# The first norm of a one-layer hybrid encoder: loads, weight splits and tensor work in a new order

## The chip, the cores and the metric

The kernel runs on one core of a Trainium2 chip. The metric is device time in microseconds (us) of one execution; it is given as the median of three runs. A hardware profile of one further execution gives the trace: what each engine did and when, and what ended each wait. The engines are PE (TensorE matmul; PEld is its weight load), ACT (ScalarE), DVE (VectorE), POOL (GpSimd) and SP (SyncE, which here only issues loads and stores). PE's clock has two levels, 1.2 and 2.4 GHz, which the profile shows as a granted clock of 0.50 and 1.00.

## What is computed

512 prompt tokens and 64 sample tokens with 1024 channels go through one transformer-like layer. The change touches only its beginning:

```python
def ada_modulation(c, w_ada, b_ada):
    mod = jax.nn.silu(c) @ w_ada + b_ada           # 6 vectors of 1024 for prompt, 6 for sample
    return jnp.split(mod[:, None, :], 6, axis=-1)  # sh1, sc1, g1, sh2, sc2, g2

h = rms_norm(x, norm1_g) * (1 + sc1) + sh1
q, k, v, qi, ki, wi, ga, gb = jnp.split(h @ w_in, PROJ_SPLITS, axis=-1)
u = ga * jax.nn.sigmoid(gb)                        # feeds a causal depthwise convolution, width 31
```

What follows is sparse attention with an indexer, the convolution, an output projection, a second norm and a squared-ReLU MLP of width 4096.

## The kernel before

All 576 tokens are held at once, channels on the partitions, in eight tiles `hat` of 128 channels. Weights keep fp32 accuracy by a split: `hi` is the rounded weight (an ACT copy, L106) and `lo` the rest (a subtraction, L115, on DVE or POOL); activations `h` are split in the same way, and each product is three matmuls (hi by hi, lo by hi, hi by lo) of 288 columns.

The first stage, up to about 58 us, does the first norm and the first three products. In order:

- Five token tiles `xtok` are loaded. `rms` takes each one's mean square (ACT, L261, L262) and scales it (DVE, L263, L264); `turn_in` transposes it on PE (L272) into `hat`. `columns` brings the conditioning vectors and the small parameter rows into columns (L214, L218).
- The shift and scale of the norm come in five blocks of channels (`BLOCKS`: 2, 2, 2, 1 and 1 tiles of 128). `load_block(b)` loads four `ada` tiles of `w_ada`, `mod_steps` multiplies them (L234), copies the result (`modrow`, L106), sums and turns it (L241) and finishes it on DVE (L248, L251). `front(b)` is a generator that does this and then, one tile at a time, `modulate(k)`: `h` hi on ACT (L283), the full value on DVE (L284), `h` lo on DVE (L115).
- `products(k, m...)` multiplies `h` tile k with weight m (L415): m = 0 is the indexer key `ki` (72 columns), m = 1 the gate `gb0`, m = 2 the value `ga0`. There are 8 x 3 such products of 6 matmuls each; below, (k, m) names one. `first_w(m, eng)` makes the split of weight m.
- `conv_setup` turns the convolution's taps (`small`) on PE (L426, L431) and copies them out.

PE, ACT and DVE run in the order in which the code is written (a manual schedule); POOL's order was left to a scheduler. All loads go through SP's queue in program order. Eight semaphores serve SP's loads in turn, so a load is issued only when the one eight places ahead of it has landed. The `ada` tiles rotate through `ADA` = 10 buffers, the `xtok` tiles have buffers of their own. The order of the stage is written out by hand: `step` takes a list in which an integer b advances `front(b)` by one step and a tuple (k, m...) runs `products`.

Behind the stage, `evac_ki` (L110, L106, L115) and the gate (`sig` L533, `u` L538) empty the six result banks, and the taps of the first convolution group, `yc` on DVE (L562, L564), start from `u`. `wraw`, `whi` and `wlo` are the weights of the products that follow (L290 to L292), split by `split`.

Of the kernel before, what the change touches and what calls it, by code (L numbers as in the profile page):

```python
# [7 lines left out]
FT = mybir.dt.float32  # L8
# [4 lines left out]
OP = mybir.AluOpType  # L13
AX = mybir.AxisListType

D = 1024
# [15 lines left out]
NP_ = 4  # L32
KP = FF // 128 // NP_
W = 31
ADA = 10
VEC, PEC = (0, 3), (1, 2)

P = dict(PRW=30, TPE=5, CS0=43, KYW=5, TAP=2, T0=20, IDX=2, TKS=12, ATT=4, SMP=6, MOD=21, CPW=15, MODL=6, S0=4, KEYW=5, TAPW=8, SCW=14, MODW=20, QIW=6, CSW=16, TKW=9, TK2=2, TKP=2, ATW=6, SMW=6, TT=3, CN1=8, CN2=21, CN3=8, RT=3, CNW=17)
HALO = W - 1
# [4 lines left out]
EPS = 1e-6  # L44
# [27 lines left out]
def step_kernel(ctx: ExitStack, tc: tile.TileContext, io):  # L72
    nc = tc.nc
    act, dve, pool, pe = nc.scalar, nc.vector, nc.gpsimd, nc.tensor

    def new_pool(stack, name, bufs=1):
        return stack.enter_context(tc.tile_pool(name=name, bufs=bufs, reuse_waits="tile"))

    cst = new_pool(ctx, "cst")
# [15 lines left out]
    def p_lg():  # L95
        return bank("lg", 2)

    def p_tp():
        return bank("tp", 2)
# [21 lines left out]
    def xtile(i):  # L121
        return (x_p[128 * i:128 * i + 128], 128) if i < 4 else (x_s, SAMP)

    start = ExitStack()
    stp = new_pool(start, "start")

    rows = stp.tile([128, 128], FT, name="rows")
    crow = stp.tile([16, 128], FT, name="crow")
    for s, ap in enumerate((io["c_prompt"], io["c_sample"])):
# [3 lines left out]
    xt = []  # L133
    for i in range(5):
        src, n = xtile(i)
        t = stp.tile([128, D], FT, name=f"xtok{i}")
        nc.sync.dma_start(t[:n], src)
        xt.append((t, n))
        for r, ap in parts[2 * i:2 * i + 2]:
            k = ap.shape[1] // 128  # L140
            nc.sync.dma_start(rows[r:r + k, :], ap.rearrange("o (n c) -> (o n) c", c=128))

    BLOCKS = ((0, 2), (2, 2), (4, 2), (6, 1), (7, 1))

    def load_block(b):
        f0, nf = BLOCKS[b]
        tiles = []
        for v in range(2):
            for kh in range(2):
                t = stp.tile([128, 4, 256], FT, name="ada", tag="ada", bufs=ADA)[:, :, :128 * nf]  # L150
                c0 = 1024 * v + 128 * f0
                nc.sync.dma_start(t, w_ada[512 * kh:512 * kh + 512, c0:c0 + 128 * nf].rearrange("(k p) c -> p k c", p=128))
                tiles.append(t)
        return tiles
# [3 lines left out]
    def load_w(name, src, r0, c0, n=128):  # L158
        raw = wgt.tile([128, NK, 128], FT, name="wraw", tag="wraw", bufs=3)
        nc.sync.dma_start(raw[:, :, :n], src[r0:r0 + 1024, c0:c0 + n].rearrange("(k p) c -> p k c", p=128))  # L160
        wraw[name] = (raw, n)
# [8 lines left out]
        return hi, lo, n  # L170

    small = stp.tile([128, 2, 512], FT, name="small")
    pool.memset(small[:, 0], 0.0)
    pool.memset(small[:64, 1], 0.0)
    ada = [load_block(0)]
    load_w("ki", w_in, 0, C_KI, 72)
    for s in range(4):
        n = 8 if s < 3 else 7
        nc.sync.dma_start(small[32 * s:32 * s + n, 0], io["conv_w"][0][s:s + 4 * n - 3:4])
    nc.sync.dma_start(small[:W, 1], io["conv_w"][0])  # L180
    nc.sync.dma_start(small[32:32 + HALO, 1], io["state_conv"][0, 0])
    load_w("gb0", w_in, 0, C_GB)
    ada.append(load_block(1))
    load_w("ga0", w_in, 0, C_GA)
    for b in (2, 3, 4):
        ada.append(load_block(b))


    begin = ExitStack()
    begin.enter_context(tc.manual_schedule(engines={mybir.EngineType.PE, mybir.EngineType.Activation, mybir.EngineType.DVE}))  # L190
    ident = cst.tile([128, 128], FT, name="ident")
    par = cst.tile([128, 128], FT, name="par")
    ones = cst.tile([128, 128], FT, name="ones")
    onec = cst.tile([128, 128], FT, name="onec")
    eps = cst.tile([128, 1], FT, name="eps")
    jp = stp.tile([128, 128], FT, name="jp")
    pool.iota(jp, pattern=[[1, 128]], base=0, channel_multiplier=-1, allow_small_or_imprecise_dtypes=True)
    dve.tensor_scalar(ident, jp, 0.0, None, op0=OP.is_equal)
    pa = mt([128, 128], FT, "pa")
    dve.tensor_scalar(pa, jp, 64.0, None, op0=OP.is_equal)  # L200
    dve.tensor_scalar(par, jp, -64.0, None, op0=OP.is_equal)
    dve.tensor_tensor(par, par, pa, op=OP.add)
    dve.tensor_tensor(par, par, ident, op=OP.add)
    pool.memset(ones, 1.0)
    pool.memset(onec, 1.0 / 512.0)
    pool.memset(eps, EPS)

    cs = cst.tile([128, NK, 32], FT, name="cs")
    pool.memset(cs, 0.0)
    cols = cst.tile([128, 128], FT, name="cols")  # L210

    def columns():
# [179 lines left out]
    def first_w(m, eng):  # L392
        hl = [stp.tile([128, NK, 128], FR, name=f"fw{m}{z}") for z in range(2)]
        fw[m] = split_w(("ki", "gb0", "ga0")[m], *hl, eng=eng)
# [28 lines left out]
    def conv_setup():  # L423
        t = p_tp()
        for c in range(4):
            pe.transpose(t[:, 64 * c:64 * c + 64], small[:64, 1, 128 * c:128 * c + 128], ident[:64, :64])  # L426
        tv = t[:, :256].rearrange("p (c j) -> p c j", c=4)
        t = p_lg()
        for b in range(16):
            for s in range(4):  # L430
                pe.matmul(t[32 * s:32 * s + 32, 8 * b:8 * b + 8], lhsT=small[:, 0, 32 * b:32 * b + 32],  # L431
                          rhs=ident[:, 32 * s:32 * s + 8], start=True, stop=True, tile_position=(0, 32 * s), skip_group_check=True)
        yield
        copy_to(act, cw, tv[:, :, :W])
        copy_to(act, us[:, :, :HALO], tv[:, :, 32:32 + HALO])
        copy_to(act, wcol, t[:, :128])
        dve.tensor_tensor(i4, ident[:, 0:32], ident[:, 32:64], op=OP.add)
        dve.tensor_tensor(i4, i4, ident[:, 64:96], op=OP.add)
        dve.tensor_tensor(i4, i4, ident[:, 96:128], op=OP.add)
# [12 lines left out]
    def step(*todo):  # L452
        if not banks:
            banks.extend([p_acc(), p_acc(), p_acc(), p_lg(), p_lg(), p_av()])
        for e in todo:
            if isinstance(e, int):
                next(fr[e])
            else:
                products(*e)

    next(fr[0])
    first_w(0, pool)
    next(fr[0])
    setup = conv_setup()
    next(setup)
    first_w(1, pool)
    step((0, 0), 0)
    next(setup, None)
    step((1, 0), (0, 1))
    first_w(2, dve)  # L470
    step(1, (1, 1), 1, 1, (0, 2), (1, 2), (2, 0, 1, 2), (3, 0))
    step(2, (3, 1), 2, 3, 2, (3, 2), 3, (4, 0, 1, 2))
    fetch()
    fetch()
    ckr = big.tile([128, 8, 2, 64], FT, name="ckr", tag="b")
    for s in range(2):
        nc.sync.dma_start(ckr[:, :, s, :], io["cache_kidx"][0, 0].rearrange("(n p) d -> p n d", p=128))
    step(4, (5, 0), 4)
    split()
    step((5, 1), (5, 2), (6, 0), (7, 0))  # L480
    for j in range(2):
        evac_ki(j, banks[j][:, :HALF], JS[j])
    step((6, 1), (7, 1), (6, 2), (7, 2))
# [821 lines left out]
    for part in range(NP_ - 1):  # L1305
        a_ = first_layer(part)
        for m in range(NK):
# [3 lines left out]
            else:  # L1311
                for r in JS:
                    t = p_ff()[:, :HALF]
# [45 lines left out]
    for m in range(2, NK):  # L1359
        ws.append(weight())  # L1360
        t = p_ff()[:, :320]
# [49 lines left out]
```

## Time and profile before

| What | Value |
|---|---|
| Median of 3 runs | 861.04 us (860.79 to 861.17) |
| The profiled execution | 860.36 us |
| Its span, first to last instruction | 858.6 us |
| PE busy | 808.2 us, 94% of the span |
| DVE, ACT, POOL busy | 449.0, 412.5, 303.5 us |
| Granted PE clock, mean | 0.973 |
| DMA, mean | 111 GB/s |

The span is what the trace covers; the profiled execution is 1.8 us longer than its span and 0.7 us shorter than the median. A busy PE is not a PE at its peak: at the lower clock it is as busy with half the work.

### The profile page before, as it was taken

What the parts mean: (1) busy time and instruction counts of PE and PEld (TensorE: products, weight loads), DVE (VectorE), ACT (ScalarE), POOL (GpSimd) and SP (SyncE); (2) the same over time, 40 slices, a digit from 0 to 9 for tenths busy, and PEclk for the clock granted to TensorE, in tenths of its full rate; (3) what the DMA queues carried; (4) which work ended last, traced back from release to release, by engine and by line L of the source; (5) the groups of instructions that cost most, each with busy time, mean ns of one, the idle gap of its engine ahead of it and who ended that gap; (6) DMA issues with size and microseconds to landing.
All of it is one profiled execution on the core that took longest, in us unless ns stands there. A gap on an engine that the chain in (4) does not pass through costs nothing.

```text
span 858.6 us, 17186 instructions
## 1 busy us (share of the span) xinstructions
PE 808.2 (94%) x6787; PEld 753.0 (88%) x6787; DVE 449.0 (52%) x1148; ACT 412.5 (48%) x976; POOL 303.5 (35%) x337
## 2 busy tenths in 40 slices
PE   5998997989798999999999999999999999999995
PEld 3797895567777988989999999999999999999995
DVE  4569879999997444654934311343113321144142
ACT  5365554555776787754745411443224522244332
POOL 0146342222244414232424343343433343343800
PEclk8799999899999999999999999999999999999998
DMA  8984157247343343732222323223222323223312
GB/s 241 309 205 123 53 146 184 60 100 187 112 113 110 116 137 115 222 122 77 74 74 75 97 76 93 80 75 99 74 77 82 88 83 90 74 74 101 120 55 57
DMA packets 164555, 95.57 MB, mean 111 GB/s; under 512 B 7699, under 2 KB 161119, under 8 KB 164475
## 3 DMA queue, kind: packets, MB, share of 16 engines
q1 hardware_dynamic: 164475, 94.48, 39.2%
q8 instruction: 53, 0.87, 0.4%
q14 instruction: 27, 0.22, 0.1%
HBM read 88.82 MB, written 5.64 MB: 110 GB/s over the span
## 4 chain that ended last, share of the span: by engine, by line
PE 69%; DVE 17%; ACT 7%; DMA 3%; issue 3%; POOL 1%; SPq 0%; ACTq 0%; DVEq 0%; POOLq 0%
PE ps_acc L290 11%; PE ps_acc L291 11%; PE ps_acc L292 11%; PE ps_lg L292 5%; PE ps_lg L290 5%; PE ps_lg L291 5%; DVE yc L564 3%; PE ps_av L292 3%; PE ps_av L290 2%; PE ps_av L291 2%; DVE score L690 2%; DVE m L688 2%; PE ps_tp L234 2%; DMA ada<-w_ada 1%; PE ps_av L887 1%
## 5 line engine op out<-in xcount | busy, mean ns | idle before, releaser
L332 POOL TENSOR_TENSOR wlo<-wraw,whi 128x512 fp32r<-128x512 f32 x172 | 222.6, 1314 | 378.3 <-ACT whi L106 378.0
L290 PE MATMUL ps_acc<-h,whi 128*128 128x288 f32 (+1 forms) x608 | 190.8, 314 | 0.0
L291 PE MATMUL ps_acc<-h,whi 128*128 128x288 f32 (+1 forms) x608 | 181.7, 299 | 0.0
L292 PE MATMUL ps_acc<-h,wlo 128*128 128x288 f32 (+1 forms) x608 | 181.1, 298 | 0.0
L106 ACT ACTIVATE whi<-wraw 128x512 fp32r<-128x512 f32 x172 | 99.8, 621 | 126.4 <-issue 120.6
L290 PEld LDWEIGHTS ps_acc<-h,whi 128*128 128x128 f32 x608 | 116.2, 191 | 14.3 <-issue 12.4
L291 PEld LDWEIGHTS ps_acc<-h,whi 128*128 128x128 f32 x608 | 116.7, 192 | 0.8
L292 PEld LDWEIGHTS ps_acc<-h,wlo 128*128 128x128 f32 x608 | 116.3, 191 | 0.0
L1266 ACT ACTIVATE z<-z,bs 128x224 f32<-128x224 f32 (+2 forms) x96 | 40.2, 450 | 98.6 <-DVE z L1262 98.6
L1087 DVE SCALAR_TENSOR_TENSOR x<-ps_acc,mod,x 128x288 f32<-128x288 f32 (+3 forms) x91 | 36.2, 420 | 83.6 <-PE ps_acc L292 83.0
L564 DVE SCALAR_TENSOR_TENSOR yc<-u,cw,yc 128x606 f32<-128x606 f32 x60 | 58.4, 981 | 0.6
L292 PE MATMUL ps_acc<-a,wlo 128*128 128x288 f32 x192 | 56.7, 295 | 0.0
L290 PE MATMUL ps_acc<-a,whi 128*128 128x288 f32 x192 | 56.6, 295 | 0.0
L291 PE MATMUL ps_acc<-a,whi 128*128 128x288 f32 x192 | 56.6, 295 | 0.0
L292 PE MATMUL ps_lg<-h,wlo 128*128 128x288 f32 (+1 forms) x176 | 52.2, 296 | 0.8 <-POOL wlo L332 0.8
L291 PE MATMUL ps_lg<-h,whi 128*128 128x288 f32 (+1 forms) x176 | 52.2, 297 | 0.0
L290 PE MATMUL ps_lg<-h,whi 128*128 128x288 f32 (+1 forms) x176 | 52.2, 296 | 0.1
L747 ACT ACTIVATE gc<-sful,sg 128x544 bf16<-128x544 f32 x48 | 35.8, 746 | 28.6 <-DVE sg L745 27.8
L872 POOL TENSOR_SCALAR prob<-prob,mx 128x128 f32<-128x128 f32 (+3 forms) x32 | 20.2, 631 | 56.8 <-DVE mx L871 34.2
L1087 DVE SCALAR_TENSOR_TENSOR x<-ps_lg,mod,x 128x64 f32<-128x64 f32 (+4 forms) x34 | 12.7, 407 | 52.5 <-PE ps_lg L292 52.5
L292 PE MATMUL ps_lg<-a,wlo 128*128 128x288 f32 x128 | 37.8, 295 | 0.0
L290 PE MATMUL ps_lg<-a,whi 128*128 128x288 f32 x128 | 37.8, 295 | 0.0
(358 smaller groups left out, 2019.0 us busy)
## 6 DMA issues: line engine op xcount, KB each, us to landing
wraw<-w_ff SPq DMA_DIRECT2D x64, 512.0 KB
ada<-w_ada SPq DMA_DIRECT2D x44, 512.0 KB
wraw<-w_in SPq DMA_DIRECT2D x24, 512.0 KB
wraw<-w_out SPq DMA_DIRECT2D x8, 512.0 KB
rep<-ud SPq DMA_DIRECT2D x24, 115.0 KB
xtok<-x_prompt SPq DMA_DIRECT2D x4, 512.0 KB
ada<-w_ada SPq DMA_DIRECT2D x8, 256.0 KB
ct<-cache_k SPq DMA_DIRECT2D x8, 256.0 KB
```

The costliest lines, as they stand in the source:

```text
L106: act.activation(out, in_, AF.Copy, scale=1.0 if scale is None else scale)
L234: pe.matmul(t[r:r + 32, :w], lhsT=cs[:, 4 * kh + kk, :], rhs=operand(v, kh, kk), start=kk == 0, stop=kk == 3, tile_position=(0, r))
L290: pe.matmul(out, lhsT=hi, rhs=src[:, 0, cs_], start=first, stop=False)
L291: pe.matmul(out, lhsT=hi, rhs=src[:, 1, cs_], start=False, stop=False)
L292: pe.matmul(out, lhsT=lo, rhs=src[:, 0, cs_], start=False, stop=last)
L332: behind[0] = pool.tensor_tensor(lo[:, c], raw[:, c], f(hi[:, c]), op=OP.subtract).ins
L564: dve.scalar_tensor_tensor(yc[c], src, w, yc[c], op0=OP.mult, op1=OP.add)
L688: dve.max(m, score[i])
L747: act.activation(eq, sful, AF.Sign, bias=cands[:, z:z + 1], scale=-1.0, accum_out=cnts[:, z:z + 1])
L872: pool.tensor_scalar(pt[:, :n], pt[:, :n], m[:, 1:2], 1.0, op0=OP.mult, op1=OP.mult)
L1087: dve.scalar_tensor_tensor(xm[:, a:b], t[:, a - r.start:b - r.start], mod[:, g, s, m:m + 1], xm[:, a:b], op0=OP.mult, op1=OP.add)
L1266: act.activation(y, y, AF.Relu, bias=bs[:, s:s + 1])
```

## The change

Everything is in the first stage. The constants (`ident`, `ones` and others) are made first, and POOL joins the engines that run in written order. The `xtok` tiles share the `ada` buffers, of which there are now 15. Parameter rows and convolution taps are loaded through POOL's queue. `gb0` is loaded directly behind `ki`. All three first weights are split on DVE. `conv_setup` moves from the beginning to between the last products of tile 4 and the first of tile 5, and takes its second bank from `p_tp`. A helper `warm(n)` runs n matmuls of `ones` by `ones` whose result nobody reads. The list of steps is written anew.

```diff
-ADA = 10
+ADA = 15
...
-    begin.enter_context(tc.manual_schedule(engines={mybir.EngineType.PE, mybir.EngineType.Activation, mybir.EngineType.DVE}))
+    begin.enter_context(tc.manual_schedule(engines={mybir.EngineType.PE, mybir.EngineType.Activation, mybir.EngineType.DVE,
+                                                     mybir.EngineType.Pool}))
...
-        t = stp.tile([128, D], FT, name=f"xtok{i}")
+        t = stp.tile([128, D], FT, name=f"xtok{i}", tag="ada", bufs=ADA)
         nc.sync.dma_start(t[:n], src)
         xt.append((t, n))
         for r, ap in parts[2 * i:2 * i + 2]:
             k = ap.shape[1] // 128
-            nc.sync.dma_start(rows[r:r + k, :], ap.rearrange("o (n c) -> (o n) c", c=128))
+            pool.dma_start(rows[r:r + k, :], ap.rearrange("o (n c) -> (o n) c", c=128))
...
     ada = [load_block(0)]
     load_w("ki", w_in, 0, C_KI, 72)
-    for s in range(4):
-        n = 8 if s < 3 else 7
-        nc.sync.dma_start(small[32 * s:32 * s + n, 0], io["conv_w"][0][s:s + 4 * n - 3:4])
-    nc.sync.dma_start(small[:W, 1], io["conv_w"][0])
-    nc.sync.dma_start(small[32:32 + HALO, 1], io["state_conv"][0, 0])
     load_w("gb0", w_in, 0, C_GB)
     ada.append(load_block(1))
     load_w("ga0", w_in, 0, C_GA)
     for b in (2, 3, 4):
         ada.append(load_block(b))
...
+    for s in range(4):
+        n = 8 if s < 3 else 7
+        pool.dma_start(small[32 * s:32 * s + n, 0], io["conv_w"][0][s:s + 4 * n - 3:4])
+    pool.dma_start(small[:W, 1], io["conv_w"][0])
+    pool.dma_start(small[32:32 + HALO, 1], io["state_conv"][0, 0])
...
-        t = p_lg()
+        t = p_tp()
         for b in range(16):
             for s in range(4):
                 pe.matmul(t[32 * s:32 * s + 32, 8 * b:8 * b + 8], lhsT=small[:, 0, 32 * b:32 * b + 32],
...
+    def warm(n):
+
+        t = p_tp()
+        for _ in range(n):
+            pe.matmul(t[:, :128], lhsT=ones, rhs=ones, start=True, stop=True)
+
+    first_w(0, dve)
     next(fr[0])
-    first_w(0, pool)
+    warm(3)
     next(fr[0])
+    warm(6)
+    first_w(1, dve)
+    step((0, 0), 0)
+    first_w(2, dve)
+    step((0, 1, 2), 1, (1, 0), 1, 1, (1, 1, 2), (2, 0, 1, 2), 2, (3, 0), 2, 2, (3, 1, 2), (4, 0), 3, (4, 1), 3, (4, 2))
     setup = conv_setup()
     next(setup)
-    first_w(1, pool)
-    step((0, 0), 0)
+    step((5, 0))
     next(setup, None)
-    step((1, 0), (0, 1))
-    first_w(2, dve)
-    step(1, (1, 1), 1, 1, (0, 2), (1, 2), (2, 0, 1, 2), (3, 0))
-    step(2, (3, 1), 2, 3, 2, (3, 2), 3, (4, 0, 1, 2))
+    step(4)
...
-    step(4, (5, 0), 4)
+    step((5, 1, 2), 4, (6, 0), (7, 0))
     split()
-    step((5, 1), (5, 2), (6, 0), (7, 0))
```

Three places show how the order moves. First SP's queue in the kernel before, from the last token tile on (`ada` are tiles of the blocks, `wraw` with 72 columns is `ki`, the next two `wraw` are `gb0` and `ga0`):

```order
L137 DMA xtok_94<-x_sample 64x1024
L152 DMA ada<-w_ada 128x4x256 x4
L160 DMA wraw<-w_in 128x8x72
L179 DMA small<-conv_w 8x512 x3
L179 DMA small<-conv_w 7x512
L180 DMA small<-conv_w 31x512
L181 DMA small<-state_conv 30x512
L160 DMA wraw<-w_in 128x8x128
L152 DMA ada<-w_ada 128x4x256 x4
```

The same place in the changed kernel:

```order
L158 DMA xtok_112<-x_sample 64x1024
L173 DMA ada<-w_ada 128x4x256 x4
L181 DMA wraw<-w_in 128x8x72
L181 DMA wraw<-w_in 128x8x128
L173 DMA ada<-w_ada 128x4x256 x4
```

The six loads of taps that stood between `ki` and `gb0` have gone to POOL's queue; `ga0` still stands behind block 1. Second, PE from block 0's modulation to block 1's in the kernel before (fw_295 and fw_296 are hi and lo of `ki`, fw_382 and fw_383 those of `gb0`):

```order
L234 MATMUL ps_tp<-ada,cs 32x256 x16
L241 MATMUL ps_tp<-sel,modrow 128x4 x2
L426 MATMUL ps_tp<-ident,small 128x64 x4
L431 MATMUL ps_lg<-ident,small 32x8 x64
L415 MATMUL ps_acc<-h,fw_295 72x288
...
L415 MATMUL ps_acc<-h,fw_382 128x288
L415 MATMUL ps_acc<-h,fw_383 128x288
...
L234 MATMUL ps_tp<-ada,cs 32x256 x16
```

In the changed kernel fw_276 and fw_277 are `ki`, fw_323 and fw_324 `gb0`, fw_346 and fw_347 `ga0`:

```order
L235 MATMUL ps_tp<-ada,cs 32x256 x16
L466 MATMUL ps_tp<-ones 128x128 x3
L242 MATMUL ps_tp<-sel,modrow 128x4 x2
L466 MATMUL ps_tp<-ones 128x128 x6
L416 MATMUL ps_acc<-h,fw_276 72x288
...
L416 MATMUL ps_lg<-h,fw_346 128x288
L416 MATMUL ps_lg<-h,fw_347 128x288
L416 MATMUL ps_av<-h,fw_346 128x288
...
L235 MATMUL ps_tp<-ada,cs 32x256 x16
```

The setup is gone from here, the `ones` matmuls are in, and `ga0` is now read before block 1's modulation, where it was first read after it. Third, PE around the setup's new place, from the last `ga0` product of tile 4 to the last block's turning:

```order
L416 MATMUL ps_av<-h,fw_346 128x288
L427 MATMUL ps_tp<-ident,small 128x64 x4
L432 MATMUL ps_tp<-ident,small 32x8 x64
L416 MATMUL ps_acc<-h,fw_276 72x288
...
L235 MATMUL ps_tp<-ada,cs 32x128 x16
...
L242 MATMUL ps_tp<-sel,modrow 128x4
```

All three products of tile 5 now stand ahead of that last turning; in the kernel before, only its `ki` product did, and no setup stood there.

## Rows read from the trace of the kernel before

**Rows 1.** The profile's page, part 1: busy time, share of the span, instructions.
```profile
PE 808.2 (94%) x6787; PEld 753.0 (88%) x6787; DVE 449.0 (52%) x1148; ACT 412.5 (48%) x976; POOL 303.5 (35%) x337
```
**Rows 2.** Stretches: PE, PEld, DVE, ACT, POOL busy (count); PE clock, DMA share, GB/s.
```profile
2.50:13.50 11.00, 5.36 (x24) 4.70 (x24) 4.27 (x11) 6.38 (x15) 0.18 (x1) 1.00 0.96 267
13.50:17.50 4.00, 2.52 (x20) 1.70 (x18) 3.48 (x8) 3.94 (x10) 0.00 (x0) 0.95 1.09 348
...
19.50:21.00 1.50, 1.50 (x16) 0.78 (x20) 0.00 (x0) 0.00 (x0) 0.00 (x0) 0.50 0.42 103
...
19.50:33.30 13.80, 11.99 (x180) 8.40 (x180) 6.44 (x12) 4.55 (x10) 3.84 (x2) 0.50 1.00 304
...
24.00:34.00 10.00, 8.67 (x161) 7.05 (x165) 6.44 (x12) 4.38 (x10) 3.84 (x2) 0.50 1.09 341
34.50:58.00 23.50, 23.50 (x258) 20.97 (x251) 13.42 (x36) 12.32 (x25) 3.89 (x4) 1.00 0.83 215
...
61.00:98.00 37.00, 32.48 (x240) 30.36 (x238) 36.14 (x53) 17.93 (x43) 20.96 (x34) 0.95 0.48 130
```
**Rows 3.** PE's timeline: start, us, line, out<-in, count, idle time before it and releaser.
```profile
13.93 0.28 PE L218 MATMUL ps_tp<-ident,rows 76*128 76x76 f32 x1
...
19.49 3.62 PE L234 MATMUL ps_tp<-ada,cs 128*32 128x256 f32 x26 [0.57 <-DMA ada<-w_ada]
...
24.53 0.69 PE L426 MATMUL ps_tp<-ident,small 64*128 64x64 f32 x4
25.14 1.89 PE L431 MATMUL ps_lg<-ident,small 128*32 128x8 f32 x128
26.97 2.28 PE L415 MATMUL ps_acc<-h,fw 128*72 128x288 f32 x8
...
33.35 2.31 PE L234 MATMUL ps_tp<-ada,cs 128*32 128x256 f32 x32
...
38.52 0.96 PE L415 MATMUL ps_acc<-h,fw 128*72 128x288 f32 x6
...
41.84 1.93 PE L234 MATMUL ps_tp<-ada,cs 128*32 128x256 f32 x32
```
**Rows 4.** ACT's timeline, same columns.
```profile
25.64 1.15 ACT L283 ACTIVATE h<-hat,mod 128x512 fp32r<-128x512 f32 x2 [1.54 <-DVE mod L251]
...
33.32 1.06 ACT L106 ACTIVATE fw<-wraw 128x1024 fp32r<-128x1024 f32 x1 [4.07 <-DMA wraw<-w_in]
...
53.41 2.18 ACT L106 ACTIVATE whi<-wraw 128x512 fp32r<-128x512 f32 x4
...
58.83 0.41 ACT L533 ACTIVATE sig<-ps_lg 128x288 f32<-128x288 f32 x1
```
**Rows 5.** DVE's timeline, same columns.
```profile
27.50 2.80 DVE L284 TENSOR_SCALAR hfull<-hat,mod 128x512 f32<-128x512 f32 x2
...
34.41 1.22 DVE L115 TENSOR_TENSOR fw<-wraw,fw 128x1024 fp32r<-128x1024 f32 x1 [2.69 <-ACT fw L106]
...
37.48 0.77 DVE L284 TENSOR_SCALAR hfull<-hat,mod 128x512 f32<-128x512 f32 x2
...
51.90 0.23 DVE L248 TENSOR_TENSOR mod<-ps_tp,cols 128x2 f32<-128x2 f32 x2 [0.40 <-PE ps_tp L241]
...
61.22 1.09 DVE L562 TENSOR_SCALAR yc<-u,cw,cols 128x606 f32<-128x606 f32 x1
```
**Rows 6.** POOL's timeline, same columns.
```profile
27.82 2.44 POOL L115 TENSOR_TENSOR fw<-wraw,fw 128x1024 fp32r<-128x1024 f32 x1 [2.23 <-ACT fw L106]
```
**Rows 7.** SP's timeline, same columns: the issue of `gb0`'s load.
```profile
19.46 0.39 SPq L160 DMA_DIRECT2D wraw<-w_in  x1
```
**Rows 8.** PE's timeline after an idle stretch later in the program.
```profile
84.85 0.44 PE L622 MATMUL ps_lg<-kip,qi 128*128 128x384 f32 x1 [1.70 <-ACT relu L625]
...
85.97 0.44 PE L290 MATMUL ps_acc<-h,whi 128*128 128x288 f32 x1
...
89.37 0.29 PE L290 MATMUL ps_acc<-h,whi 128*128 128x288 f32 x1
```

More of the change, by code (lines that the diff above doesn't have):

```diff
@@ L125, in step_kernel @@
     stp = new_pool(start, "start")
+    begin = ExitStack()
+    begin.enter_context(tc.manual_schedule(engines={mybir.EngineType.PE, mybir.EngineType.Activation, mybir.EngineType.DVE,
+                                                     mybir.EngineType.Pool}))
+    ident = cst.tile([128, 128], FT, name="ident")
+    par = cst.tile([128, 128], FT, name="par")
+    ones = cst.tile([128, 128], FT, name="ones")
+    onec = cst.tile([128, 128], FT, name="onec")
+    eps = cst.tile([128, 1], FT, name="eps")
+    jp = stp.tile([128, 128], FT, name="jp")
+    pool.iota(jp, pattern=[[1, 128]], base=0, channel_multiplier=-1, allow_small_or_imprecise_dtypes=True)
+    dve.tensor_scalar(ident, jp, 0.0, None, op0=OP.is_equal)
+    pa = mt([128, 128], FT, "pa")
+    dve.tensor_scalar(pa, jp, 64.0, None, op0=OP.is_equal)
+    dve.tensor_scalar(par, jp, -64.0, None, op0=OP.is_equal)
+    dve.tensor_tensor(par, par, pa, op=OP.add)
+    dve.tensor_tensor(par, par, ident, op=OP.add)
+    pool.memset(ones, 1.0)
+    pool.memset(onec, 1.0 / 512.0)
+    pool.memset(eps, EPS)
     rows = stp.tile([128, 128], FT, name="rows")
@@ L172, in step_kernel @@
     small = stp.tile([128, 2, 512], FT, name="small")
-    pool.memset(small[:, 0], 0.0)
-    pool.memset(small[:64, 1], 0.0)
     ada = [load_block(0)]
     load_w("ki", w_in, 0, C_KI, 72)
-    for s in range(4):
-        n = 8 if s < 3 else 7
-        nc.sync.dma_start(small[32 * s:32 * s + n, 0], io["conv_w"][0][s:s + 4 * n - 3:4])
-    nc.sync.dma_start(small[:W, 1], io["conv_w"][0])
-    nc.sync.dma_start(small[32:32 + HALO, 1], io["state_conv"][0, 0])
     load_w("gb0", w_in, 0, C_GB)
@@ L186, in step_kernel @@
         ada.append(load_block(b))
-    begin = ExitStack()
-    begin.enter_context(tc.manual_schedule(engines={mybir.EngineType.PE, mybir.EngineType.Activation, mybir.EngineType.DVE}))
[L191 to L206, printed above, removed]
     cs = cst.tile([128, NK, 32], FT, name="cs")
     pool.memset(cs, 0.0)
+    pool.memset(small[:, 0], 0.0)
+    pool.memset(small[:64, 1], 0.0)
+    for s in range(4):
[3 more added lines that the diff above has]
+    pool.dma_start(small[32:32 + HALO, 1], io["state_conv"][0, 0])
     cols = cst.tile([128, 128], FT, name="cols")
```

## The prediction

> **What bounds the kernel now.** The page's first part says that PE is busy 94% of the span [rows 1]. That is a mean, and the change lies in the first 58 us, so I read that stretch alone: first the stretches, then the timelines of PE, ACT and DVE.
>
> The stretches [rows 2] show three regimes. From 2.5 to 13.5 us the token tiles arrive at 267 GB/s with a DMA share of 0.96; from 13.5 to 17.5 us block 0 comes at 348 GB/s with a share of 1.09. Then there is a hole: from 19.5 to 21 us 103 GB/s and a share of 0.42. The queue explains it: between `ki` and `gb0` stand six small loads of taps, and `gb0` is issued only at 19.46 us [rows 7], with block 1 behind it. From 24 to 34 us the rate is 341 GB/s again. From 34.5 to 58 us PE is busy 23.50 of 23.50 us at the full clock. So up to about 33 us the stage is bound by what has landed, and from there by PE.
>
> PE's timeline [rows 3] gives the marks. Block 0's modulation waits for its last tile until 19.49. The convolution setup runs from 24.53 to 27.03 (0.69 and 1.89 us, at clock 0.50). The first product starts at 26.97, and the `h` that it reads was made by ACT from 25.64 for 1.15 us, to 26.79 [rows 4]: the setup filled a wait and cost some 0.2 us. Block 1's modulation starts at 33.35, and then PE never rests. `ga0` has landed at 33.32, where ACT stops waiting for it [rows 4], and its lo part is ready at 35.63 (34.41 plus 1.22) [rows 5]; PE has other work until then.
>
> What the stage hands on is not PE's last product but the last tile's modulation. It starts when DVE gets the last sums, at 51.90 [rows 5]. From there ACT makes `h`, splits weights (53.41), empties banks and gates, up to `sig` at 58.83, which ends at 59.24 [rows 4], and DVE starts the taps `yc` at 61.22 [rows 5]. From 61 to 98 us DVE is busy 36.14 of 37.00 us, while PE has 4.5 us idle [rows 2]. So a delay of the mark at 51.90 goes through DVE into the end almost whole. I forecast that mark.
>
> **The change part by part.** *Constants first, buffers, POOL's order.* The first token tile lands after the constants are made in either order, so this is worth nothing on the path. The 15 buffers hold the five token tiles and ten block tiles, as many block tiles as before; the eleventh now waits for a token tile that has long been used, not for block 0's matmuls. That moves blocks 2 to 4 forward, which PE did not wait for: nothing.
>
> *Small loads on POOL's queue.* They are 0.23 MB, and 11 of them were on SP between the first token tile and `gb0`. No row shows a load issued by POOL. The parameter rows are needed by PE at 13.93 [rows 3]; the six issues start at about 2 us, so even 1.5 us each leaves room: I take nothing, with a loss of 1 us at most if they come late. The tap loads are not needed until the setup, some 20 us later than before.
> The Trainium skill, page "DMA: Bandwidth & Descriptors", section "Issuing engines are not separate DMA queues", says that loads from different engines run on the same 16 DMA engines and that a second issuer saves only issue time. By it the 0.23 MB still cost what they did, and only the hole at 19.5 us, which is an issue wait, would go. The trace shows that hole, and shows no overlap of two issuers.
>
> *When `ga0` lands.* Order behind the token tiles: block 0, `ki` (0.29 MB), `gb0` (0.52), block 1 (2.10), `ga0` (0.52). Block 0 was complete at 19.49. Without small loads between the token tiles, at most the lacking share (0.96 against 1.09, 12% of 11 us, 1.3 us) is won: it lands at 18.2 to 19.5, and I take 18.9. Behind it come 3.43 MB. At 348 GB/s they take 9.9 us. At the slow end, in the kernel before 304 GB/s for 13.8 us moved 4.20 MB up to `ga0`, where 3.6 were ahead of it: 0.6 MB of later tiles overtook. With these too, at 341 GB/s, it is 11.8 us [rows 2]. I take 10.6, nearer the fast end, since part of the overtaking comes from the hole. So `ga0` lands at 29.5, between 28.1 and 31.3: some 3.8 us earlier than before.
>
> *The new wait.* PE now reads `ga0` with tile 0, ahead of block 1's modulation. By then it has done (0, 0) and most of (0, 1), so it stands. Behind the waiting matmul on PE is all that is left; on ACT behind the copy of `ga0` stands block 1's `modrow`, on DVE behind the subtraction stand block 1's sums. After landing, the copy takes 1.06 and the subtraction 1.22 us [rows 4, 5], 2.3 together. PE goes on in full at 31.8.
>
> *What PE has to do up to the mark.* Before, from 33.35 to 51.90, 18.55 us without a pause: four modulations, four turnings, and 78 of the 144 product matmuls (18 were done, 48 left). After, from 31.8: the same four and four, but 97 product matmuls, 7 left of tile 0 and all 90 of tiles 1 to 5. 24 of them and nothing else ran from 38.52 to 41.84, 0.138 us each [rows 3], so the 19 more cost 2.6 us. The setup now stands in a full stretch: 2.5 us at the half clock before, 1.25 if all of it scales; I take 1.6. At (4, 0) the lo part comes late by some 0.3 us, since only 12 matmuls (1.66 us) stand between the turning and it, and the way through DVE and ACT takes 2.4. Against that, block 1's modulation ran 2.31 us where block 2's ran 1.93, the rest of a low clock: 0.4 less. Sum: 18.55 + 2.6 + 1.6 + 0.3 - 0.4 = 22.65. The mark comes at 31.8 + 22.65 = 54.45, which is 2.55 us late.
>
> *What is taken off.* POOL's splits go (2.44 us for `gb0` [rows 6]), and with them the DVE step beside them of 2.80 us that takes 0.77 elsewhere [rows 5]. This delayed tile 1, which now waits for `ga0` anyway: no gain left. `warm` puts nine matmuls around block 0's turning; they end before `ga0` lands: no cost, and PE's clock is likely up by then.
>
> *Behind the mark*, (7, 0) has only (6, 0) in front and PE stands about 1 us; ACT's chain is longer, so it costs nothing more.
>
> **Sum.** 860.36 + 2.55 = 862.9 for the profiled execution; the median is 0.7 above it, so 863.6. With `ga0` at 28.1 it is 862.2, at 31.3 it is 865.4; a setup of 1.25 or 2.5 us moves it by -0.35 or +0.9.
>
> **Rivals.** *The loads ran slowly because of how they were issued, and now run at full rate from the start: faster.* From the start of the token tiles at 2.5 us, 7.84 MB up to `ga0` at 348 GB/s end at 25.0. For it speaks the rate between 13.5 and 17.5, against it the share of 0.96 up to 13.5: the DMA engines were busy, only slow. The mark then comes at 25.0 + 2.3 + 22.65 = 49.95, 1.95 early: 859.1. No change is reached with `ga0` at 27.0, and 0.2% is gained from 25.2 down. Chance 0.18.
>
> *Both sides cancel.* `ga0` between 25.2 and 28.6, the order's loss eaten by the closed hole: 861.0. For it speaks that the hole is plain in the rows. Chance 0.27.
>
> *The clock falls while PE waits for `ga0`.* PE stands for some 2 to 3 us around 29 to 32. Later in the program, after an idle time of 1.70 us, its 288-column matmuls take 0.44 instead of 0.29 us from 84.85 until before 89.37 [rows 8]: at most 4.5 us at the lower level of the clock, a loss of at most 2.2, and I take 1.8. Here that comes on top: 865.4. Against it, that stretch had more idle time around it than the one row shows. Chance 0.17.
> The Trainium skill, page "TensorE: Matmul & The Clock Gate", section "HAM oscillation — how this bites in real kernels", tells of this: a wait for a load lets the clock fall, and the next work starts slow. The trace agrees at 84.85 us, with 0.44 against 0.29 us [rows 8].
>
> **How the numbers follow.** The forecast has 0.38, the three rivals 0.18, 0.27 and 0.17. 0.2% of 861 is 1.7 us, about what a measurement of this kernel can tell from no change, so slower begins at 862.8 and faster ends at 859.3. Slower takes the third rival and 0.35 of the forecast, 0.52; faster takes nearly all of the first, 0.17; the same is left with 0.31. The likeliest case alone lies between 862.2 and 865.4. Eight in ten need both neighbours: from 859.8, which leaves out most of the first rival, to 866.0.
>
> **What the changed profile would show.** Right: no hole of DMA before block 1, and 300 GB/s or more between block 0 and `ga0`; ACT's wait for `ga0` ends near 29.5; PE idle 2 to 3 us in front of the first `ga0` products; the setup in 1.3 to 2 us at full clock; the last block's sums on DVE at 54 to 55, `yc` at about 63.8. Wrong: `ga0` landed by 27, no idle time of PE there, the mark at or before 52, or DVE not full from 61 to 98, so that the delay is swallowed.

## The result and the profile after

The changed kernel takes 867.62 us, median of four executions (867.17 to 868.48), the kernel before 861.11 in the same series: ratio 1.0076, 95% interval 1.0059 to 1.0094. It is slower by 6.5 us, where 2.5 were forecast; the range ended at 866.0. The profiled execution is the one of 868.48 us, span 866.7.

The page's first part, as [rows 1], and the stretches that answer to [rows 2], same columns; the last one is 61 to 98 us moved by the 6.1 us that DVE is late:

```profile
PE 808.0 (93%) x6805; PEld 752.5 (87%) x6805; DVE 446.4 (52%) x1150; ACT 412.9 (48%) x976; POOL 307.4 (35%) x347
```
```profile
2.50:13.50 11.00, 5.59 (x26) 5.23 (x27) 4.90 (x10) 7.73 (x18) 6.94 (x14) 1.00 1.05 309
...
19.50:21.00 1.50, 1.50 (x24) 0.73 (x13) 0.22 (x1) 0.83 (x2) 0.00 (x0) 1.00 1.18 295
19.50:30.30 10.80, 5.97 (x54) 4.23 (x42) 5.35 (x11) 4.20 (x7) 0.00 (x0) 0.86 1.12 331
24.00:34.00 10.00, 3.40 (x14) 2.42 (x13) 4.35 (x6) 2.71 (x4) 0.00 (x0) 0.67 1.11 338
...
67.10:104.10 37.00, 30.67 (x238) 28.68 (x236) 36.14 (x53) 17.85 (x41) 22.08 (x36) 1.00 0.49 131
```

The loads did better: 309 GB/s up to 13.5 us (267 before), and the hole at 19.5 us is closed (295, was 103). But PE did 14 matmuls between 24 and 34 us, at a mean clock of 0.67; it had done 161 there, 132 of them the setup's small ones. DVE is as full behind the stage as it was: 36.14 of 37 us. PE's timeline shows the place:

```profile
18.90 1.91 PE L235 MATMUL ps_tp<-ada,cs 128*32 128x256 f32 x26 [0.92 <-DMA ada<-w_ada]
...
26.17 0.42 PE L416 MATMUL ps_lg<-h,fw 128*128 128x288 f32 x2
31.42 0.61 PE L416 MATMUL ps_lg<-h,fw 128*128 128x288 f32 x1 [4.83 <-ACT fw L106]
32.68 0.61 PE L416 MATMUL ps_lg<-h,fw 128*128 128x288 f32 x1 [0.65 <-DVE fw L115]
...
34.66 3.36 PE L235 MATMUL ps_tp<-ada,cs 128*32 128x256 f32 x32
...
43.36 1.93 PE L235 MATMUL ps_tp<-ada,cs 128*32 128x256 f32 x32
...
52.51 0.46 PE L427 MATMUL ps_tp<-ident,small 64*128 64x64 f32 x4
52.89 1.26 PE L432 MATMUL ps_tp<-ident,small 128*32 128x8 f32 x128
```

Block 0 is complete at 18.90. Then PE stands 4.83 us for ACT's copy of `ga0` and 0.65 us for its lo part, and what follows runs at the lower clock (granted 1.00 from 21 to 27.3 us, 0.50 from 27.4 to 37.6): the first matmul takes 0.61 us (0.40 in e3 below, at the full clock), block 1's modulation 3.36, block 2's, with as many matmuls, 1.93. ACT's and DVE's rows, as [rows 4, 5]: `ga0` landed at 30.31, its lo part, and the mark (the last block's sums) with what starts from it:

```profile
30.31 1.06 ACT L106 ACTIVATE fw<-wraw 128x1024 fp32r<-128x1024 f32 x1 [4.66 <-DMA wraw<-w_in]
```
```profile
31.40 1.23 DVE L115 TENSOR_TENSOR fw<-wraw,fw 128x1024 fp32r<-128x1024 f32 x1 [3.98 <-ACT fw L106]
...
58.05 0.23 DVE L249 TENSOR_TENSOR mod<-ps_tp,cols 128x2 f32<-128x2 f32 x2 [3.38 <-PE ps_tp L242]
...
67.36 1.09 DVE L570 TENSOR_SCALAR yc<-u,cw,cols 128x606 f32<-128x606 f32 x1
```

The mark is 6.15 us late (58.05 against 51.90), `yc` 6.14 late (67.36 against 61.22): it is handed on whole. Further on the profiled execution loses more. PE's timeline there:

```profile
104.50 0.44 PE L630 MATMUL ps_lg<-kip,qi 128*128 128x384 f32 x1 [3.05 <-ACT relu L633]
...
106.02 0.63 PE L630 MATMUL ps_lg<-kip,qi 128*128 128x512 f32 x1
...
106.87 0.44 PE L291 MATMUL ps_acc<-h,whi 128*128 128x288 f32 x1
```

In the kernel before, the clock fell at 85 us [rows 8], and PE then waited 1.59 us at this place. Here it did not fall at 85, PE came early, waited 3.05 us, and the clock fell behind that wait, on the path: DVE's instructions are 6.0 us late up to 100 us and 7.5 from 109 us on. That is one execution (868.48 us, 8.1 above the profiled one before); the median of +6.5 is close to the 6.15 of the mark alone.

### The profile page after: what moved, and what is told of

It reads as the page before. It is cut to its first block, busy times and chain, and to the rows that moved or that the text cites. A ratio compares the mean times of both kernels' runs of the same rounds, so it can differ in the third digit from the quotient of the medians.

```text
span 866.7 us, 17233 instructions
## 1 busy us (share of the span) xinstructions
PE 808.0 (93%) x6805; PEld 752.5 (87%) x6805; DVE 446.4 (52%) x1150; ACT 412.9 (48%) x976; POOL 307.4 (35%) x347
## 4 chain that ended last, share of the span: by engine, by line
PE 68%; DVE 16%; ACT 7%; issue 3%; SPq 2%; DMA 2%; POOL 1%; ACTq 0%; DVEq 0%; POOLq 0%
PE ps_acc L291 11%; PE ps_acc L292 11%; PE ps_acc L293 11%; PE ps_lg L293 5%; PE ps_lg L291 5%; PE ps_lg L292 5%; DVE yc L572 3%; DVE score L698 3%; PE ps_av L293 3%; PE ps_av L291 2%; PE ps_av L292 2%; DVE m L696 2%; PE ps_tp L235 2%; DMA wraw<-w_in 1%; ACT gc L755 1%
```

## Experiments

Each is given with the time of the kernel before in its own series and the ratio with its interval. "Mark" is the start of the last sums on DVE in the profile: 51.90 before, 58.05 changed. It is read from one execution each: with the changed kernel's loads as they are, ACT's wait for `ga0` ended between 29.59 (e9) and 30.77 us (e5), so a difference of less than about 1 us between two marks shows little by itself.

**e1 and e2: the loads alone, the order alone.** e1 is the changed kernel with the old list of steps (with it POOL's splits, the setup's old place and bank, no `warm`); e2 is the kernel before with the new list and what belongs to it. From e1's edit:

```diff
-    first_w(0, dve)
     next(fr[0])
-    warm(3)
+    first_w(0, pool)
...
-    step((0, 1, 2), 1, (1, 0), 1, 1, (1, 1, 2), (2, 0, 1, 2), 2, (3, 0), 2, 2, (3, 1, 2), (4, 0), 3, (4, 1), 3, (4, 2))
+    step((1, 0), (0, 1))
+    first_w(2, dve)
+    step(1, (1, 1), 1, 1, (0, 2), (1, 2), (2, 0, 1, 2), (3, 0))
```

> The changed kernel's loads (constants first, 15 buffers, small loads on POOL's queue, gb0 ahead of block 1) with PE's written order, the POOL splits and the early setup of the kernel before, without warm. Theory (the new order loses, because PE stands for ga0 with its clock falling, and because more work stands ahead of the last turning; the loads themselves gain a little): block 1 lands near 28.5 us, PE starts its modulation about 1 to 2 us earlier than at 33.35, so 859 to 861 us. Rival (the loads or POOL's queue are what costs): 864 us or more.

> The kernel before with only the written order of the changed one: DVE splits, warm, ga0's products of tile 0 ahead of block 1, late setup; its loads stay on SP's queue with the hole at 19.5 us. Theory: ga0 lands near 33.3 us instead of 30.3, the wait is 3 us longer and the clock is low all through it: 869 to 872 us, slower than the changed kernel. Rival (the loads cost): 861 to 864 us.

e1: 861.0 us (859.61 to 862.32) against 860.47, ratio 1.0006 (0.9996 to 1.0017), mark 50.57. e2: 868.95, ratio 1.0102 (1.0086 to 1.0117), mark 60.27. So the loss lies in the order, and none of it in the loads. The loads bring `ga0` to 30.2 us in e1 and gain 1.3 us at the mark, nothing that the time shows.

**e3, e4 and e9: the wait for `ga0`.** e3 puts 18 matmuls of `ones` into it; e4 moves `ga0`'s split and tile 0's product behind block 1's modulation; e9 leaves out `warm`.

The beginnings of the list of steps, e3's and e4's (the lists go on as changed):

```diff
-    step((0, 1, 2), 1, (1, 0), 1, 1, (1, 1, 2),
+    step((0, 1))
+    warm(18)
+    step((0, 2), 1, (1, 0), 1, 1, (1, 1, 2),
```
```diff
-    first_w(2, dve)
-    step((0, 1, 2), 1, (1, 0), 1, 1, (1, 1, 2),
+    step((0, 1), 1)
+    first_w(2, dve)
+    step((1, 0), 1, 1, (0, 2), (1, 1, 2),
```

> The changed kernel with 18 more matmuls of ones by ones (0.25 us each at full clock, 4.5 us) between the products (0, 1) and (0, 2), so that PE is busy while it waits for ga0; the wait itself stays. Theory (2.4 us of the loss is the clock that falls during the wait): clock 1.00 from 27 to 38 us, block 1's modulation 1.9 instead of 3.4 us, the last sums at 55.6 instead of 58.05: 865.2 us. Rival (the clock is a bystander): 867.6 us.

> The changed kernel with ga0's split and its products of tile 0 moved behind block 1's modulation; loads, warm, late setup and the tail as they are. Theory (the wait for ga0 and the clock are the larger part): block 1 lands near 28.5 us, its modulation starts then instead of at 34.66, the last sums come at 52 to 53: 861.5 to 863 us. Rival (the tail is the larger part, setup and tile 5 ahead of the last turning): not under 865 us.

> The changed kernel without its 9 x 2 matmuls of ones around block 0's turning. Theory: they end before ga0 lands and PE's clock falls in the wait for ga0 with them or without them, so the last sums stay at 58 us and the time at 867.6, within 0.8. Rival: they keep the clock up through the first products, and without them the low stretch begins earlier and is longer: first products at half clock, 2 to 3 us later, of which the wait for ga0 hides most; the block 1 modulation would still be at half clock; 868.5 or more.

e3: 866.1 us (864.41 to 867.88), ratio 1.0070 (1.0050 to 1.0089). Its PE timeline, then its DVE timeline:

```profile
33.12 0.40 PE L416 MATMUL ps_lg<-h,fw 128*128 128x288 f32 x1 [0.86 <-DVE fw L115]
...
33.97 1.93 PE L235 MATMUL ps_tp<-ada,cs 128*32 128x256 f32 x32
```
```profile
56.15 0.23 DVE L249 TENSOR_TENSOR mod<-ps_tp,cols 128x2 f32<-128x2 f32 x2 [3.70 <-PE ps_tp L242]
```

With the clock at 1.00 the way from `ga0`'s lo part to the mark is 56.15 - 33.12 = 23.03 us, in the changed kernel 58.05 - 32.68 = 25.37. The low clock cost 2.3 us. The time shows less, 0.5 us by the two ratios, whose intervals overlap: in its profiled execution e3 is 4.3 us behind the kernel before up to 100 us, and 7.0 behind at the end, with a fall of the clock at 102 us.

e4: 862.51 us (861.0 to 866.14), ratio 1.0026 (1.0012 to 1.0039), mark 52.95. So the place of `ga0` is 5.1 of the 6.15 us at the mark, and in time 4.5 of the 6.5 (each against the kernel before of its own series). e9: 866.19 against 860.28, ratio 1.0070 (1.0055 to 1.0085), mark 56.39. `warm` gains nothing that shows here: the ratios differ by less than their intervals. The mark is 1.66 us earlier than in the changed kernel, where no change was expected: `ga0` was there 0.7 us earlier, and block 1's modulation took 2.50 us instead of 3.36, since the clock rose at 35.1 us instead of 37.6.

**e8: the small loads on SP's queue again**, between the token tiles and between `ki` and `gb0`.

```diff
-            pool.dma_start(rows[r:r + k, :], ap.rearrange("o (n c) -> (o n) c", c=128))
+            nc.sync.dma_start(rows[r:r + k, :], ap.rearrange("o (n c) -> (o n) c", c=128))
...
     load_w("ki", w_in, 0, C_KI, 72)
+    for s in range(4):
+        n = 8 if s < 3 else 7
+        nc.sync.dma_start(small[32 * s:32 * s + n, 0], io["conv_w"][0][s:s + 4 * n - 3:4])
...
     load_w("gb0", w_in, 0, C_GB)
```

> The changed kernel with the rows and taps loaded through SP's queue again, between the token tiles and between ki and gb0. Theory: the move to POOL's queue is what closed the hole at 19.5 us and brought ga0 from 33.3 to 30.3; put back, ga0 lands at 32.5 to 33.5, and since PE waits for it, the last sums come 2.2 to 3 us later, at 60.3 to 61, and the time is 870. Rival: gb0's earlier place and the extra buffers are what brought ga0 forward, and the queue is worth nothing: ga0 stays near 30.5 and the time at 867.6.

868.9 us (868.05 to 870.54) against 860.28, ratio 1.0098 (1.0081 to 1.0115), mark 61.16, `ga0` at 33.80. The hole is back in its stretches:

```profile
2.50:13.50 11.00, 5.36 (x24) 4.59 (x24) 3.64 (x9) 5.43 (x12) 0.27 (x2) 1.00 0.98 273
19.50:21.00 1.50, 0.82 (x8) 0.40 (x12) 0.00 (x0) 0.00 (x0) 0.00 (x0) 0.50 0.13 26
```

POOL's queue is worth 3.5 us for `ga0` and 3.1 at the mark. The 0.23 MB themselves are 0.8 us at 300 GB/s. SP issued `gb0`'s load at 20.15 us here and at 11.58 in the changed kernel, `ga0`'s at 24.93 and at 20.82: the rest fits SP's waiting.

**e10, e5 and e7: the end of the stage.** e10 puts only the last turning back ahead of tile 5's later products; e5 puts the setup back early too; e7 is e5 with e4's place of `ga0`.

All three, and then e5 and e7 (in which the late setup goes, and block 4's modulation stands ahead of (5, 0)):

```diff
-    step((5, 1, 2), 4, (6, 0), (7, 0))
+    step(4, (5, 1, 2), (6, 0), (7, 0))
```
```diff
     warm(3)
     next(fr[0])
+    setup = conv_setup()
+    next(setup)
     warm(6)
     first_w(1, dve)
     step((0, 0), 0)
+    next(setup, None)
```

> The changed kernel with one thing put back: the last block's turning again ahead of the m = 1 and m = 2 products of tile 5; the setup stays late. e5 could not show the worth of the tail, since its setup took both turning banks and held PE up early. Theory: the last sums come 12 matmuls, 1.66 us, earlier, at 56.4 us, and what follows hangs on them: 866.0, between 865 and 867. Rival: the stage's end hangs on PE's work as a whole, which is unchanged, and the time stays at 867.6.

> The changed kernel with only its end of the stage put back: the setup stands again behind block 0's turning, and the last block's turning ahead of the m = 1 and m = 2 products of tile 5. Theory: the tail is a plain sum on a PE that has no idle time there, so the last sums come earlier by the setup (1.57 us) and by 12 matmuls (12 x 0.138 = 1.66 us), at 54.8 us instead of 58.05, and the time is some 3.2 us below the changed kernel's 867.6: 864.4, between 863.3 and 865.6. The setup in its old place costs nothing, since PE waits for ga0 behind it anyway. Rival: the early setup delays the first products and the wait for ga0 does not absorb it, so that only 1.7 us come back: 866. Second rival: what follows hangs on PE's last product, not on the last sums, and nothing comes back beyond the setup's share: 866 too, but with the last sums at 54.8.

> The tail put back as in e5 and ga0's products behind block 1's modulation as in e4, all else as changed. Theory: the two losses add. e4 had its last sums at 52.95 us; less 3.2 us is 49.7, which is 2.2 us ahead of the kernel before (51.90). If that goes to the end it is 859 us; as e1 had its last sums 1.33 us early and no measurable gain, I allow up to 860.5. Rival: once ga0 no longer stops PE, the early setup stands in a stretch that is full, and costs its 1.57 us there instead: last sums at 51.3, 860.5 to 861.

e10: 865.48 us (865.32 to 867.8) against 861.16, ratio 1.0058 (1.0037 to 1.0078), mark 57.44. The last turning now waits 0.46 us for `modrow`, and block 1's modulation took 3.64 us, 0.3 more: the mark is 0.6 us earlier, or 0.9 without that 0.3, where 1.66 were expected. e5: 866.38 (860.38 to 867.4), ratio 1.0056 (1.0036 to 1.0077), mark 55.69, not 54.8. e7: 865.99, ratio 1.0068 (1.0051 to 1.0086), mark 57.15, neither 49.7 nor the rival's 51.3. In e5 and e7 `warm`'s bank waited 2.4 us for the setup's copies (a fault of these two edits, not of the change), and then PE stood 2.4 us with the releaser "issue": it waited for nothing that the profile shows.

**e11, e12 and e14: the stop.** e11 is e7 with the setup's second bank from `p_lg` and behind `warm(6)`, so that nothing waits for its copies. e12 has block 1 loaded ahead of `gb0`, an early setup and an order made for that. e14 is e11 with the setup late, as changed.

e11 against e7, and e12's loads:

```diff
-        t = p_tp()
+        t = p_lg()
         for b in range(16):
...
+    warm(6)
     setup = conv_setup()
     next(setup)
-    warm(6)
```
```diff
     load_w("ki", w_in, 0, C_KI, 72)
+    ada.append(load_block(1))
     load_w("gb0", w_in, 0, C_GB)
-    ada.append(load_block(1))
```

> e7 with its setup in the bank that the kernel before used (of p_lg), behind the second group of ones matmuls instead of ahead of it, so that nothing waits for the setup's copies: ga0's products behind block 1's modulation, setup early, last turning ahead of tile 5's later products; the changed kernel's loads. Theory: the losses found so far are all of the change, and they add: e4's last sums at 52.95 less 1.57 and 1.66 give 49.7, 2.2 us ahead of the kernel before, so 858.0 to 859.5 where the kernel before gives 860.3. Rival: an early setup costs its time where ga0 no longer stops PE: last sums at 51.3, 860 to 860.5. Second rival: as in e1, a lead at the last sums is lost again behind it: 860.5 whatever the last sums say.

> A version made for the cause found: PE must never stand at a weight ahead of work that has landed. The changed kernel's loads, with block 1 ahead of gb0 and ga0; block 1's modulation behind the ki products of tiles 0 and 1; gb0's products from tile 0 on as its lo part comes, ga0's last; the setup early; the last turning ahead of tile 5. Block 1 lands 0.52 MB earlier, about 26.5 us; from 30 us on PE has no wait, and the last sums come at 45 to 48 us, 4 to 7 us ahead of the kernel before. Theory: all of the lead goes to the end as every delay did: 854 to 857. Rival: the loads of blocks 2 to 4, which land until 42 us, hold the last sums at 48 to 50: 857 to 859. Second rival: what follows the stage waits for its own weights, so that a lead beyond 2 us is lost: 859 or more.

> e11 with the setup in its late place again, as the changed kernel has it; nothing else differs but the bank. Theory: without the early setup PE's 218th matmul comes at about 40 us, long after its piece of program, so the stop of 4.48 us goes; PE waits for block 1 until 28.8 and the last sums come at 52.95 - 1.66 = 51.3 us, 3.2 us ahead of e11 although the setup now stands in the path: 860.5, between 859.5 and 861.5. Rival: the stop is a load effect and comes in any order: last sums at 54.5 plus the setup, 56, and 865.

e11: 864.34 us (860.78 to 866.75) against 861.16, ratio 1.0042 (1.0028 to 1.0057), mark 54.48. e12: 864.63, ratio 1.0044 (1.0026 to 1.0061), mark 54.47. Both forecasts failed, and most of what they missed is one stop of PE. PE's timeline of e11, and its stretches up to the end of the stop and within it:

```profile
23.87 1.17 PE L432 MATMUL ps_lg<-ident,small 128*32 128x8 f32 x118
29.53 0.33 PE L432 MATMUL ps_lg<-ident,small 128*32 128x8 f32 x10 [4.48 <-issue]
```
```profile
0.00:29.52 29.52, 14.80 (x218) 11.90 (x219) 14.46 (x36) 16.83 (x35) 8.72 (x23) 0.96 1.00 287
24.90:29.50 4.60, 0.15 (x16) 0.05 (x7) 3.00 (x7) 1.16 (x4) 0.00 (x0) 0.77 1.12 329
```

PE stops between two alike instructions of the setup, the next with all its operands in place. It has done 218 matmuls. The trace's DMA records show what landed before it went on: a packet of 16 KB of a queue of kind "instruction". The same for the other traces, in us (the 92nd is that weight load's start):

| Kernel | 92nd weight load | packet | matmuls done | PE goes on | stop |
|---|---|---|---|---|---|
| before | 25.22 | 27.96 to 29.09 | 218 | 30.48 | 1.23 |
| e1 | 21.90 | 25.46 to 26.59 | 218 | 28.07 | 1.48 |
| e5 | 24.55 | 28.39 to 29.61 | 217 | 30.93 | 2.40 |
| e7 | 24.14 | 28.12 to 29.31 | 217 | 30.70 | 2.37 |
| e11 | 22.72 | 26.89 to 28.07 | 218 | 29.53 | 4.48 |
| e12 | 22.45 | 26.21 to 27.42 | 218 | 28.83 | 4.73 |
| changed | 22.64 | 25.91 to 27.07 | 218 at 45 us | | none |

Order and time differ, the count stays at 217 or 218; PE goes on 1.3 to 1.5 us behind the packet's end; the packet starts 2.7 to 4.2 us behind the 92nd weight load, in all 18 traces (a count of 90 to 96 fits about as well). The page of the kernel before has 53 packets in that queue (0.87 MB), and PE has 6787 matmuls and as many weight loads: 256 to a packet. The reading of these figures is that PE's program comes in pieces by DMA while the weights load, and that one lasts for some 126 matmuls (218 less 92). A setup of 132 small ones, run in 1.6 us, uses a piece up before the next is there. e13 to e16 test that reading.
The Trainium skill, page "Runtime: NRT & Kernel Launch", section "Instruction fetch mechanics", says that an engine's program streams in blocks of 16 KiB or 256 instructions, and that this is mostly hidden. The size agrees (a 16 KB packet; 126 matmuls with their weight loads are 252); hidden it was not, at 1.23 to 4.73 us.

e14: 862.54 us (860.5 to 864.4) against 861.14, ratio 1.0016 (1.0005 to 1.0027), mark 51.89, no stop, as expected of the count; the rival, a stop by the load in any order, fell. The time is 1 us above the range expected. e14 differs from e11 in the setup's place and bank, and is 2.6 us earlier at the mark although the setup now stands on the path. It is also e4 with e10's tail: the two bring the mark from 58.05 over 52.95 to 51.89, where the kernel before has it, so they account for the whole 6.15 us.

**e13 and e15: the setup ahead of block 0's modulation**, where PE waits for block 0, with e12's and with e14's order, and without `warm`.

> e12 with its setup moved ahead of block 0's modulation, where PE waits for block 0 (15.4 to 18.9 us) and the taps have landed at 15.96, and without ones matmuls. In six runs PE stopped after its 217th or 218th matmul, at a time between 23.8 and 28.6 us, and went on 1.3 to 1.5 us after a 16 KB packet of the instruction queue; that packet began 2.7 to 4.3 us after PE's 91st matmul in all runs. Theory: PE's program comes in pieces through the same DMA engines, a piece lasts for some 128 matmuls, and a setup of 132 that takes 1.6 us uses one up before the next is there. Here the 91st matmul comes at about 16.6 us, the next piece about 6 us later, at 22.7, and the 218th matmul only at 23: almost no stop. Block 1 lands at 26, PE is full from about 30, last sums at 44 to 47 us, 853 to 856 us. Rival: it is not the count of matmuls but the load on the DMA engines between 24 and 30 us that stops PE, whatever its program: a stop of over 2 us there again, last sums at 50 or later, 859 or more.

> e14 with the setup ahead of block 0's modulation and no ones matmuls; loads in the changed kernel's order. Theory as for e13: no stop of over 1 us, the setup hidden in the wait for block 0, last sums 1.57 us ahead of e14's, at 49.7: 859. If the clock falls in front of block 1's modulation, as without ones matmuls in e9, 1 to 2 us of it are lost again: 860 to 861. Rival: the copies of the setup's result delay ACT's modrow and h, and block 0's steps come late: no gain over e14.

e13: 862.1 us (859.85 to 863.25) against 861.14, ratio 1.0006 (0.9995 to 1.0018), mark 50.59. e15: 861.31 (859.63 to 864.5), ratio 1.0005 (0.9993 to 1.0017), mark 52.47. No stop of PE in either, as the count foretold; by the rival, the load on the DMA engines, there had to be one of over 2 us. But the marks came late, and so did e13's time, 6 us above its range: in both, the setup's copies held up `ki`'s copy on ACT, behind it the sums on DVE, and so ACT's `h`, for which PE stood 2.43 us, and block 1's modulation ran in part at the lower clock (2.83 and 3.03 us); in e13 `gb0`'s copy also stood behind block 1's `modrow`, until 30.89.

**e16 and e17: the copies put earlier, and `warm` back in.**

```diff
+    setup = conv_setup()
+    next(setup)
+    next(setup, None)
     first_w(0, dve)
     next(fr[0])
     warm(3)
     next(fr[0])
     warm(6)
     first_w(1, dve)
     step((0, 0), 0)
+    step((0, 1), 1)
     first_w(2, dve)
-    step((0, 1, 2), 1, (1, 0), 1, 1, (1, 1, 2), (2, 0, 1, 2), 2, (3, 0), 2, 2, (3, 1, 2), (4, 0), 3, (4, 1), 3, (4, 2))
+    step((1, 0, 1), 1, 1, (0, 2), (1, 2), (2, 0, 1, 2), 2, (3, 0), 2, 2, (3, 1, 2), (4, 0), 3, (4, 1), 3, (4, 2))
...
-    step((5, 1, 2), 4, (6, 0), (7, 0))
+    step(4, (5, 1, 2), (6, 0), (7, 0))
```

This is e17, beside e11's bank of `p_lg` and without the late setup; e16 has `(1, 0), 1, 1, (0, 2), (1, 1, 2)` instead.

> e15 with the copies of the setup's result directly behind the setup, in front of block 0's modrow on ACT (ACT has nothing to do between 17.7 and 20 us), and with the ones matmuls around block 0's turning as in the changed kernel. Theory: e15's h of tile 0 came 2.4 us late behind those copies, and PE's clock was low from 25.8 to 32.6 us; here h comes as in e4, PE's 218th matmul falls at about 23.3 us, a little behind its piece of program, and the last sums come at 52.95 - 1.66 - 1.57 = 49.7 us, 2.2 us ahead of the kernel before; 858.5 to 860 where that gives 861. Rival: the clock falls all the same in the waits for loads, as it did in e14 from 19.1 us in an order that e4 ran at full clock: last sums at 51 to 52, 860.5 to 861.5. Second rival: the ones matmuls push the 218th matmul ahead of the program again, a stop of over 1 us at 23 us; it would be hidden by the wait for block 1 until 28.8.

> e16 with the gb0 products of tile 1 moved ahead of block 1's turning, so that 6 more matmuls stand where PE waits for ga0's parts (0.2 and 0.86 us in e4). Theory: last sums another 0.8 us earlier, at 48.9; 858 to 859.5. Rival: the turning, and with it h of tile 2, comes later by as much, and nothing is gained over e16.

e16: 859.55 us (857.31 to 860.95) against 860.69, ratio 0.9987 (0.9976 to 0.9998). e17: 858.99 (857.21 to 861.39), ratio 0.9983 (0.9973 to 0.9994), mark 49.10. They beat the kernel before by 1 to 2 us, just clear of the noise, and the changed kernel by some 8. e16's PE and DVE timelines:

```profile
22.77 1.27 PE L466 MATMUL ps_tp<-ones 128*128 128x128 f32 x9 [0.25 <-issue]
```
```profile
49.45 0.23 DVE L249 TENSOR_TENSOR mod<-ps_tp,cols 128x2 f32<-128x2 f32 x2 [0.57 <-PE ps_tp L242]
```

The mark was expected at 49.7. PE stopped after 219 matmuls; the packet ended at 21.51, PE went on 1.26 us behind it, and the stop is down to 0.25 us: the count was a usable rule. e17's step gave 0.35 us at the mark of the expected 0.8, too little to tell it from none; no run has e16's order without `warm`, whose share stays open.

## Why the prediction was wrong

**Right.** The choice of the mark, and DVE passing it on whole (6.15 to 6.14). Block 0 at 18.9 (18.90), by luck in its last digits: that was the middle of 18.2 to 19.5, and runs with the same loads have it from 18.82 (e9) to 19.46 (e3). The closed hole. The wait for `ga0` as the term that decides, PE's work up to the mark (22.65 at full clock, 23.03 in e3), the setup's 1.6, the 0.3 at (4, 0) (0.27). e4 shows the wait to be the larger part of the loss, e1 and e2 that the loss is the order's and not the loads'.

**The step that failed** is "PE's clock is likely up by then", and the 0.4 us less that went with it. The clock at 0.50 in and behind the wait was kept as a rival, with 0.17, a gain of 0.4 was put into the forecast for its not happening, and 1.8 us into the rival for it. The clock was up until 27.4 us and fell in the wait; e3 measures the cost at 2.3. The nearest row [rows 8] had the fall behind a wait of 1.70 us; the forecast itself had PE standing 2 to 3 us, and so the fall should have been the likeliest case. The wait was longer still, 4.83: PE was through with (0, 1) at 26.6 us, where the forecast had it at work until about 29. The 1.8 was too small because the clock was low for 10.2 us, 5.53 of them busy, and not for 4.5 as in the row.

**Sizes.** `ga0` landed at 30.3, not 29.5, inside the bounds given; PE went on in full 0.9 us later than forecast. Then 25.37 us of work against 22.65, of which 1.4 lie in block 1's modulation (3.36 against 1.93) and 1.0 in the seven matmuls ahead of it (1.98 us against 0.97). 0.9 and 2.7 are the 3.6 us between the forecast mark and the measured one; of the 2.7, e3 leaves 0.4 at the full clock (23.03 against 22.65). The small loads between the first token tile and `gb0` were 12, not 11 (six of rows, six of taps); no term rests on it.

**The range** failed for a reason of its own: each bound was taken alone. The low clock's 865.4 with `ga0` at its late bound (1.8 us more) is 867.2, still 0.4 short of the median measured; two effects that come from one and the same wait belong in one case.

**Not seen.** The prediction took the early setup to have "filled a wait" at 0.2 us. Behind it PE then stopped, with the releaser "issue"; PE's timeline of the kernel before:

```profile
30.48 1.98 PE L415 MATMUL ps_acc<-h,fw 128*72 128x288 f32 x6 [1.23 <-issue]
```

How much of these 1.23 us was on the path no run isolates. The late setup removes the stop; `ga0`'s wait, at the same time and longer, swallowed the gain.

**Open.** Matched with the kernel before instruction by instruction on DVE, the traces gain or lose again from 100 us on, between -1.6 (e11) and +2.9 us (e14), with falls of the clock at other places; no run isolates them. Why the 1.3 us that e1 and e13 lead by at the mark show in no median stays open too: their profiled executions keep 0.8 and 1.0 of it to the end.

## What to carry to other kernels

An engine that runs in written order must not meet a weight that is still on its way while work that has landed stands behind it: price that wait together with the low clock behind it, as one case. Read idle time whose releaser is "issue" as a possible shortage of the program: count the instructions up to it in several orders, and put a burst of many small ones where the engine waits anyway and the next piece has time to come. A lead at the end of a stage is worth what the stages behind it pass on, so read both the mark in the trace and the measured time.

## What was not expected of the hardware

PE's program is fetched while the weights load: 16 KB packets, of which the first starts 2.7 to 4.2 us behind PE's 92nd weight load and is needed at about the 218th matmul; from that weight load to PE's going on it took 5.3 to 6.8 us in the kernels that stopped. And the clock is not a function of the order: e4 and e14 run the same instructions on PE up to 44 us, but the last 26 matmuls of block 0's modulation took 1.91 us in the one and 3.56 in the other, where the granted clock was 0.50 from 19.1 to 22.5 us.
